# First layer's up projection by seven block products; residual added in DRAM; dense products cut 384 and 384

## The chip, the core and the metric

The kernel runs on one core of a Trainium2 chip. The metric is the device time of one execution in microseconds (us). TensorE (PE) multiplies, VectorE (DVE) and ScalarE (ACT) work elementwise, POOL and SP issue DMAs; 16 DMA engines move data between DRAM and SBUF. Matmul results land in eight PSUM banks.

## What is computed

A diffusion backbone of two layers, all in float32: 512 latent tokens (`SEQ`) and 256 context tokens (`CTX`) of width 1024. Each layer derives shift, scale and gate vectors from a conditioning vector (adaLN), norms and modulates the tokens, projects them into a convolution module, an attention and a two-way retention, gates and sums the three branches, applies `w_out`, and ends with a gated feed-forward part:

```python
def conv_ffn(h, w_up, dw_w, dw_b, w_down):
    gt, val = jnp.split(h @ w_up, 2, axis=-1)
    gt = dwconv(gt, dw_w, dw_b)          # 3 taps along the tokens
    return (jax.nn.silu(gt) * val) @ w_down
```

`w_up` is 1024 x 5632, half of it for `gt` and half for `val`; `w_down` is 2816 x 1024. In layer 0 this runs on all 768 tokens, in layer 1 on the 512 latent ones.

## The kernel before

Activations lie with features on the 128 partitions and tokens along the free dimension, one SBUF slot of 128 x 768 (`S`, 47 slots) for a block of 128 features. Every dense product takes three passes: weight and activation are split into a rounded high part and a low part (`hi`, `lo`), and `chunk` multiplies high x high, high x low and low x high into the same bank (`mm`, L197). A product over 768 tokens takes two matmuls a pass, of 512 and 256 columns, in two banks of the `pd` pool (four banks; the `ps` pool has the other four).

Weights come as one stream (`Stream`, L75): tiles of 128 x 1024, laid out by the host in the order of use. `issue` loads a raw tile on SP's queue into a ring of two buffers (`raw`; one early tile uses the pool `rawa`, whose two buffers are otherwise for modulation weights); `prepare` splits it on ScalarE (L107) and VectorE (L108), up to four tiles ahead of the one in use; `next` hands out columns.

Work that can lie beside the dense products is written as generators ("sides"). `tick` gives each side credit, the modelled time of a product times the side's rate (`ADAR` for adaLN), and the side emits instructions until the credit is used; `finish` emits the rest at once. What is emitted first has priority on its engine; the framework's scheduler lets a later instruction pass where an earlier one is not ready. `ada_rows` (L441) works out modulation vectors on VectorE: a row of 128 x 1024 weights (buffer `rowa`) is multiplied by the conditioning and summed, a pass of 768 and one of 256 columns for each of up to two vectors (L466). `ada_late` (L476) does the last piece of layer 0 and all six of layer 1; it runs beside layer 0's feed-forward part.

`last_chunks` ends a stage: its last output tiles are produced first for one half of the tokens and then for the other (512, then 256), so that `norm` (L521) of the first half can run under the second half's matmuls. `ffn` (L1420) then runs column group by column group: `up` multiplies 8 feature blocks for `gt` and 8 for `val`, `up_g` filters and applies Silu, `up_v` multiplies and splits the result into `hid`. After groups 8, 14 and 22 the down projection of finished groups is added into the residual `xs`, kept in SBUF (`evac`, L1480); the last cut is done by `last_chunks`. Layer 1 runs the same code on 512 tokens. `parts` (L67) cuts the tokens in two.

Of the kernel before, what the change touches and what calls it, by code (L numbers as in the profile page):

```python
# [14 lines left out]
F32 = mybir.dt.float32  # L16
F32R = mybir.dt.float32r
AF = mybir.ActivationFunctionType
# [4 lines left out]
P = 128  # L23
# [11 lines left out]
NSUB = 140  # L35
# [4 lines left out]
NSLOT = 47  # L40
# [5 lines left out]
ATTR, RETR, CONVR, ADAR = (1.0, 1.0), (1.4, 1.6), (0.4, 0.4), (0.06, 0.2, 0.25)  # L46
# [17 lines left out]
LAT = [(0, SEQ)]  # L64

# [9 lines left out]
class Stream:  # L75


    def __init__(self, k, dram, total):
        self.k, self.dram, self.limit = k, dram, total
        self.blocks = []  # L80
        self.raw = {}
# [40 lines left out]
    def next(self, key, cols, held=0):  # L122
        if self.off + cols > SUB:
            self.split.pop(self.cur, None)
            self.cur += 1
            self.off = 0
            self.prepare(min(self.cur - held, self.cur if self.kept is None else self.kept) + WB)
        hi, lo = self.split[self.cur]
        o = self.off
        self.off += cols  # L130
        self.blocks.append((key, cols))
        return hi[:, o:o + cols], lo[:, o:o + cols]

# [28 lines left out]
class Kern:  # L162
# [84 lines left out]
    def dense(self, key, xs, segs, ws=None):  # L247

        pts = [(self.dps()[:, :c], o, c) for o, c in segs]
# [226 lines left out]
    def ada_late(self, l):  # L476
        yield from self.ada_rows(l, LATE)
        yield from self.ada_rows(l + 1, (1, 0, 2, 3, 4, 5))
        self.crow = None
# [41 lines left out]
    def norm(self, l, which, xs, out):  # L521
# [3 lines left out]
        def gen(segs):  # L525
# [3 lines left out]
            for k in range(KC + 1):  # L529
# [5 lines left out]
                yield  # L535
        return gen
# [690 lines left out]
    def branch(self, bi, name, ys, segs, merged, ths=(), after_split=None, before_last=None):  # L1227
# [10 lines left out]
        for m in range(KC):  # L1238
# [3 lines left out]
            if m < lead:  # L1242
# [3 lines left out]
                pps = self.group([lambda k, m=m: (name, l, k * P, m * P) for m in range(lead)], yy, segs)  # L1246
            else:
                held, pps = [th], [self.dense(lambda k: (name, l, k * P, m * P), yy, segs)]
# [36 lines left out]
    def run(self):  # L1285
# [4 lines left out]
        self.W = Stream(self, io["wstream"], DEPTH * NSUB)  # L1290
        self.att_sp = [self.dram.tile([P, TALL], F32, name=f"attsp{i}") for i in range(4)]
        xsp = self.dram.tile([KC, P, SEQ], F32, name="xspill")
        first = self.start()
        xs = []
        for l in range(DEPTH):
# [8 lines left out]
            h2 = []  # L1304
            gen = self.layer_mixers(l, last, segs, T, xs, xsp, first, h2)
            xs, first = self.ffn(l, h2, xs, segs, T, gen, xsp)
# [17 lines left out]
    def layer_mixers(self, l, last, segs, T, xs, xsp, first, h2):  # L1324
# [58 lines left out]
        self.finish(mix)  # L1383
        if l == 0:
            self.finish(ada)
            ada = self.side(self.ada_rows(l, DVP), ADAR[1])
        self.branch(2, "w_pc", self.ret_out, segs, merged, ths)
# [22 lines left out]
        def evac(m, pts):  # L1410
            for pt, o, c in pts:
# [5 lines left out]
        return self.last_chunks(lambda m, k: ("w_out", l, k * P, m * P), mm, segs, HOLDO[l], evac,  # L1417
                                self.norm(l, 1, xs, h2), LEADO)

    def ffn(self, l, h2, xs, segs, T, gen, xsp):  # L1420
        nc = self.nc
        v = self.vecs[l]
        if l + 1 < DEPTH:
            ada = self.side(self.ada_late(l), ADAR[2])
        else:
            ada = None
        cuts = [(0, 6), (6, 12), (12, 17), (17, 22)]
# [51 lines left out]

        def evac(m, pts):  # L1480
# [16 lines left out]
        up_first(FIRST[l])  # L1497
        for c in range(FIRST[l], NFF):
# [7 lines left out]
            if c == NFF - 3 and l + 1 < DEPTH:  # L1506
                self.row_vectors(l + 1)
        if ada is not None:
            self.finish(ada)
# [3 lines left out]
        gen = self.last_chunks(key(3), [hid[c] for c in range(*cuts[3])], segs, HOLDD[l], evac_last, norm)  # L1513
# [134 lines left out]
```

## Time and profile before

| | |
|---|---|
| median of 3 runs | 2318.0 us (2317.86 to 2319.08) |
| profiled execution, its own time | 2320.54 us |
| its span in the trace | 2318.8 us |
| PE / DVE / ACT busy | 98% / 66% / 37% of the span |
| matmuls | 13650 |
| weight tiles (`raw<-wstream`) | 280 of 512 KB |

Busy times are unions over an engine's instructions. Matmuls overlap, so their pace is read from start to start. "Idle before" in a group is the time that the engine stood still ahead of its instructions. A row of windows gives the stretch, its length, then for each engine the busy us and the number of instructions, the granted clock, the busy share of the DMA engines and their rate. In a group, the first figure behind the bar is busy us, the second the mean length of one in ns.

### The profile page before, as it was taken

The page shows a single profiled execution, that of the slowest core. Times are in us where ns is not written, and L with a number is a line of the kernel's source. Part 1 is how long each engine was busy: PE and PEld are TensorE (multiplying, and loading weights), DVE is VectorE, ACT ScalarE, POOL GpSimd, SP SyncE. Part 2 cuts the span into 40 slices and gives each one's busy share as a digit, 9 for nine tenths or more (in the row PEclk, how much of TensorE's full clock was granted, in tenths as well). Part 3 has the DMA queues.
Part 4 walks back from the last instruction along what each step waited for, and adds up shares of the span by engine and source line. Part 5 has one row for each costly group of instructions (what it writes and reads, how often), then busy time and mean ns, then how long its engine had stood idle before and what let it go on. Part 6 is the DMA issues. An engine that isn't in the chain of part 4 may idle for free.

```text
span 2318.8 us, 34073 instructions
## 1 busy us (share of the span) xinstructions
PE 2278.0 (98%) x13650; PEld 1953.7 (84%) x13650; DVE 1536.5 (66%) x3150; ACT 866.7 (37%) x1481; POOL 28.4 (1%) x56
## 2 busy tenths in 40 slices
PE   6999999999999999999999999999999999999998
PEld 5888888888888888888888889888888889888887
DVE  6877959798774385746763359888697556544445
ACT  3465644332232242222122234565343434323233
POOL 0000000000000000000000000000000000000000
PEclk9999999999999999999999999999999999999999
DMA  7221111123242123423651121121123322322222
GB/s 286 101 74 53 44 56 46 46 82 128 100 153 84 46 100 109 134 84 110 215 200 64 64 91 65 37 74 60 55 72 110 136 83 91 109 92 99 100 92 72
DMA packets 63838, 221.54 MB, mean 96 GB/s; under 512 B 7584, under 2 KB 9904, under 8 KB 63680
## 3 DMA queue, kind: packets, MB, share of 16 engines
q1 hardware_dynamic: 59616, 203.64, 25.4%
q0 software_dynamic: 4064, 15.73, 2.0%
q8 instruction: 107, 1.75, 0.3%
q14 instruction: 51, 0.42, 0.1%
HBM read 212.53 MB, written 6.82 MB: 95 GB/s over the span
## 4 chain that ended last, share of the span: by engine, by line
PE 92%; DVE 5%; ACT 1%; issue 1%; DMA 0%; SPq 0%; DVEq 0%; ACTq 0%
PE pd L197 81%; PE ps L197 9%; PE ps L1149 2%; DVE wlo L108 1%; DVE cacc L598 1%; DVE ht L543 0%; PE ps L1062 0%; ACT whi L107 0%; DVE hl L555 0%; DMA x<-xt 0%; DVE qq L1097 0%; DVE sq L508 0%; DVE kb L752 0%; DVE mod L418 0%; DVE kf L752 0%
## 5 line engine op out<-in xcount | busy, mean ns | idle before, releaser
L197 PE MATMUL pd<-hh,wlo 128*128 128x512 f32 (+1 forms) x2176 | 658.9, 355 | 0.0
L107 ACT ACTIVATE whi<-raw 128x1024 fp32r<-128x1024 f32 x280 | 296.6, 1061 | 968.4 <-PE pd L197 849.3
L197 PE MATMUL pd<-hl,whi 128*128 128x512 f32 (+1 forms) x2176 | 655.7, 353 | 1.9 <-DVE hl L555 1.7
L197 PE MATMUL pd<-hh,whi 128*128 128x512 f32 (+1 forms) x2176 | 655.8, 354 | 1.4 <-DVE fy L1440 0.9
L108 DVE TENSOR_TENSOR wlo<-raw,whi 128x1024 fp32r<-128x1024 f32 x280 | 341.6, 1221 | 273.7 <-ACT whi L107 270.2
L197 PEld LDWEIGHTS pd<-hh,whi 128*128 128x128 f32 x2176 | 362.0, 189 | 63.2 <-issue 1.5
L197 PEld LDWEIGHTS pd<-hl,whi 128*128 128x128 f32 x2176 | 359.7, 188 | 61.4 <-DVE hl L555 3.8
L197 PEld LDWEIGHTS pd<-hh,wlo 128*128 128x128 f32 x2176 | 360.3, 188 | 56.0 <-issue 1.1
L598 DVE SCALAR_TENSOR_TENSOR cacc<-u,vec,cacc 128x497 f32<-128x497 f32 (+9 forms) x360 | 220.3, 648 | 2.2
L197 PE MATMUL pd<-hidh,wlo 128*128 128x512 f32 (+1 forms) x558 | 169.1, 348 | 0.0
L197 PE MATMUL pd<-hidh,whi 128*128 128x512 f32 (+1 forms) x558 | 167.9, 346 | 0.0
L197 PE MATMUL pd<-hidl,whi 128*128 128x512 f32 (+1 forms) x558 | 167.3, 345 | 0.0
L1132 ACT ACTIVATE prob<-ps,amx,qrs 128x256 f32<-128x256 f32 (+1 forms) x144 | 93.7, 655 | 91.4 <-DVE amx L1127 78.3
L197 PE MATMUL pd<-whi,hl 128*128 128x256 f32 x416 | 120.1, 289 | 4.4 <-DVE hl L555 4.4
L197 PE MATMUL pd<-whi,hh 128*128 128x256 f32 x416 | 120.5, 292 | 3.4 <-ACT hh L552 3.4
L197 PE MATMUL pd<-wlo,hh 128*128 128x256 f32 x416 | 119.5, 288 | 0.0
L1483 DVE SCALAR_TENSOR_TENSOR x<-pd,mod,x 128x512 f32<-128x512 f32 (+1 forms) x102 | 62.2, 632 | 80.8 <-PE pd L197 80.5
L466 DVE SCALAR_TENSOR_TENSOR rowa<-rowa,crow 128x768 f32<-128x768 f32 (+1 forms) x144 | 94.1, 686 | 26.8 <-DMA rowa<-wadt 26.7
L197 PEld LDWEIGHTS pd<-hidh,whi 128*128 128x128 f32 x558 | 94.9, 189 | 14.9 <-issue 0.2
L1448 DVE TENSOR_TENSOR fy<-fy,pd 128x512 f32<-128x512 f32 x66 | 37.5, 596 | 104.6 <-PE pd L197 101.5
L197 PEld LDWEIGHTS pd<-hidl,whi 128*128 128x128 f32 x558 | 93.7, 188 | 14.0 <-issue 0.2
L197 PEld LDWEIGHTS pd<-hidh,wlo 128*128 128x128 f32 x558 | 94.3, 189 | 13.1
(245 smaller groups left out, 3111.9 us busy)
## 6 DMA issues: line engine op xcount, KB each, us to landing
raw<-wstream SPq DMA_DIRECT2D x280, 512.0 KB, 3.4
rowa<-wadt SPq DMA_DIRECT2D x72, 512.0 KB, 3.7
adar<-wada SPq DMA_DIRECT2D x16, 384.0 KB, 7.3
rawa<-wada SPq DMA_DIRECT2D x8, 512.0 KB, 3.5
x<-xt SPq DMA_DIRECT2D x8, 384.0 KB, 8.1
x<-xt POOLq DMA_DIRECT2D x8, 384.0 KB, 5.1
adar<-wada SPq DMA_DIRECT2D x8, 256.0 KB, 7.0
xspill<-x POOLq DMA_DIRECT2D x8, 256.0 KB, 2.3
```

Source lines behind the costliest of these rows:

```text
L107: nc.scalar.activation(hi, r, AF.Copy)
L108: nc.vector.tensor_tensor(lo, r, hi.bitcast(F32), op=ALU.subtract)
L197: return self.nc.tensor.matmul(out, w, x, start=start, stop=stop)
L466: nc.vector.scalar_tensor_tensor(out, raw[:, a:b], 1.0, t[:, o:o + b - a], op0=ALU.mult, op1=ALU.mult, accum_out=acc[:, c, j, h:h + 1])
L598: nc.vector.scalar_tensor_tensor(acc[:, a:b], u[:, a + d:b + d], w(k), acc[:, a:b], op0=ALU.mult, op1=ALU.add)
L1132: nc.scalar.activation(pr[:, o - k0:o - k0 + c], pt[:, :c], AF.Exp, scale=rs, bias=mx[:, 2:3], accum_out=sm[:, j:j + 1])
L1149: nc.tensor.transpose(pt[:, b * P:b * P + P], pr[:, o + b * P:o + b * P + P], self.ident)
L1448: nc.vector.tensor_tensor(y[:, o:o + n], y[:, o:o + n], pt, op=ALU.mult)
L1483: nc.vector.scalar_tensor_tensor(xs[m][:, s], pt, g2[:, m, j:j + 1], xs[m][:, s], op0=ALU.mult, op1=ALU.add)
```

## The change

Layer 0's up projection is taken as a product of 2 x 2 blocks: features halved (512 each), tokens halved (384 each), and the output columns of one group halved into `gt` and `val`. Winograd's form of Strassen's scheme makes seven products in place of eight, of sums and differences of blocks. `split_tokens` makes the seven token operands, each split into high and low: 28 slots. The weight operands are made per column group: the stream holds each product's first block, and the further blocks of a sum are added into the raw tile by accumulating DMAs from a second array (`wsums`, on POOL's queue) or on VectorE from another raw tile (`up_sums`). Each product is 4 x 3 matmuls of 384 columns; X collects 11, S2, S3 and 22 one behind the other and is copied out in between, Z collects S1 and S4. Six products (11 and 12 of three groups) come before the first that needs the second token half.

The stream of layer 0 grows from 140 to 173 tiles; odd tiles of the up projection use the `rawa` buffers. The residual is stored to DRAM (`xup`), the down projection's cuts are scaled into a slot and added there by accumulating DMAs, and the sum is loaded again ahead of the last cut, which has 6 groups for 5. The modulation pieces of `ada_late` go beside `w_out` of layer 0 (layer 0's last piece and two of layer 1) and beside the branches of layer 1 (its other four). The input, gate, branch and output projections and the down cuts of layer 0 take 384 + 384 columns (`even`); the last cut keeps 512 + 256.

```diff
-NSUB = 140
+NUP = 74
+NSUB = (NUP + NFF * 7 // 2 + NFF, 140)
 START = ((0, 256, 2), (256, 256, 0), (512, 256, 4), (768, 256, 0))
 ND = 4
 RAWB, RAWA = 2, 2
 WB = 4
-NSLOT = 47
+NSLOT = 48
...
-ATTR, RETR, CONVR, ADAR = (1.0, 1.0), (1.4, 1.6), (0.4, 0.4), (0.06, 0.2, 0.25)
+ATTR, RETR, CONVR, ADAR = (1.0, 1.0), (1.4, 1.6), (0.4, 0.4), (0.06, 0.25, 0.35, 0.6)
...
+HALF = TALL // 2
+EVEN = [(0, HALF), (HALF, HALF)]
+Q = 4 * P
...
+OPS = {"11": ((0, 0),), "12": ((0, 1),), "22": ((1, 1),), "S1": ((1, 0), (1, 1)), "S3": ((0, 0), (1, 0)),
+       "S2": ((0, 0), (1, 0), (1, 1)), "S4": ((0, 1), (0, 0), (1, 0), (1, 1))}
+UPFIRST = 3
+CUTS = ((0, 4), (4, 8), (8, 12), (12, 16), (16, NFF))
+CUTAT = {5: 0, 9: 1, 13: 2, 17: 3}
+def up_order():
+    first = range(UPFIRST)
...
+    for c in range(UPFIRST, NFF):
+        out += [("11", c), ("22", c - 1), ("S4", c - 1), None, ("12", c), ("S2", c), ("S1", c), ("S3", c)]
+    return out + [("22", NFF - 1), ("S4", NFF - 1)]
...
+def up_sums():
...
+    for (name, c), (i, o) in tile.items():
+        blocks = OPS[name]
+        other = {"S2": "S1", "S4": "S2"}.get(name)
+        if other and abs(tile[other, c][0] - i) <= 3:
+            dve.setdefault(i, []).append((o, *tile[other, c]))
+        else:
+            dma.setdefault(i, []).extend((o, (c, b)) for b in blocks[1:])
+    return dma, dve
...
-            pool, tag = (self.k.apool, "rawa") if i == RAWB else (self.k.raw_pool, "raw")
+            ada = i == RAWB or (NUP < i < NSUB[0] and i % 2)
+            pool, tag = (self.k.apool, "rawa") if ada else (self.k.raw_pool, "raw")
             t = pool.tile([P, SUB], F32, tag=tag, name=f"raw{i}")
             self.k.nc.sync.dma_start(t, self.dram[i])
+            for o, block in self.dma.get(i, ()):
+                self.k.nc.gpsimd.dma_start(t[:, o:o + Q], self.sums[len(self.sum_blocks)], accum_op=ALU.add)
+                self.sum_blocks.append(block)
...
-            self.issue(i + 1)
-            r = self.raw.pop(i)
+            up = NUP <= i < NSUB[0]
+            self.issue(i + 2 if up else i + 1)
+            r = self.raw[i]
+            for o, j, a in self.dve.get(i, ()):
+                nc.vector.tensor_tensor(r[:, o:o + Q], r[:, o:o + Q], self.raw[j][:, a:a + Q], op=ALU.add)
+            self.raw.pop(i - 4, None)
...
-            self.issue(self.done + RAWB)
+            self.issue(self.done + (RAWB + 1 if up else RAWB))
...
-        return self.dense(lambda k: ("w_in", l, k * P, m * P), self.h, segs)
+        return self.dense(lambda k: ("w_in", l, k * P, m * P), self.h, even(segs))
...
+    def ada_late(self, l, parts):
+        for x in parts:
+            yield from self.ada_rows(l, x)
+            l += 1
...
+    def split_tokens(self, l, xs, ops):
...
+        def block(name, i, half, k0, segs):
+            cf, sh = self.coef[l], self.mod[l]
+            t = raw[name, i] = self.S("b")
+            for e in range(2):
+                k = k0 + 2 * i + e
+                for o, c in spans(segs):
+                    j, d = o // SEQ, slice(e * HALF + o - half, e * HALF + o - half + c)
+                    nc.vector.scalar_tensor_tensor(t[:, d], xs[k][:, o:o + c], cf[:, KC + k, j:j + 1], r[:, o:o + c],
+                                                   op0=ALU.mult, op1=ALU.mult)
+                    nc.scalar.activation(t[:, d], t[:, d], AF.Identity, bias=sh[:, 24 + k, j:j + 1])
+        def parts(name, t, i):
+            ops.setdefault(name, [None, None])[i] = self.split(t, TALL, "h")
+        def gen(segs):
+            half = segs[0][0]
+            self.sq_rstd(segs, r)
+            yield
+            if not half:
+                for name, k0 in (("11", 0), ("12", 4)):
+                    for i in range(2):
+                        block(name, i, half, k0, segs)
+                        yield
+                        parts(name, raw[name, i], i)
+                        yield
+                return
...
+            for i in range(2):
+                for name, k0 in (("u", 0), ("v", 4)):
+                    block(name, i, half, k0, segs)
+                    yield
+                u, v, b = raw["u", i], raw["v", i], raw["11", i]
+                t3[i], t2[i] = self.S("t3"), self.S("t2")
+                nc.vector.tensor_tensor(t3[i], v, u, op=ALU.subtract)
+                nc.vector.scalar_tensor_tensor(t2[i], t3[i], -1.0, b, op0=ALU.mult, op1=ALU.subtract)
+                yield
+                parts("S2", t2[i], i)
+                yield
...
+            ada = self.side(self.ada_late(l, [(2, 3, 4, 5)]), ADAR[2])
...
+            late = self.side(self.ada_late(l, [LATE, (1, 0)]), ADAR[3])
...
+        norm = self.norm(l, 1, xs, h2) if last else self.split_tokens(l, xs, h2)
+        gen = self.last_chunks(lambda m, k: ("w_out", l, k * P, m * P), mm, even(segs), HOLDO[l], evac, norm, LEADO)
+        if late:
+            self.finish(late)
...
+        cuts = [(0, 6), (6, 12), (12, 17), (17, 22)] if l else CUTS
...
+        def up_seven():
+            X, Z, g, val = {}, {}, {}, {}
+            def product(pt, name, c, start=True):
+                wh, wl = self.W.next(("up", c, OPS[name][0]), Q)
+                for k in range(4):
+                    xh, xl = (a[:, k % 2 * HALF:(k % 2 + 1) * HALF] for a in h2[name][k // 2])
+                    b = slice(k * P, k * P + P)
+                    for i, (w, x) in enumerate(((wh, xh), (wh, xl), (wl, xh))):
+                        nc.tensor.matmul(pt, w[:, b], x, start=start and k == 0 and i == 0, stop=k == 3 and i == 2,
+                                         skip_group_check=not start)
+            one, two = slice(0, HALF), slice(HALF, TALL)
+            def p11(c):
+                X[c], g[c], val[c] = self.dps()[:, :HALF], self.S("fg"), self.S("fv")
+                product(X[c], "11", c)
+                nc.scalar.activation(g[c][:, one], X[c], AF.Copy)
...
+            def s2(c):
+                product(X[c], "S2", c, False)
+                nc.scalar.activation(g[c][:, two], X[c], AF.Copy)
+            def s1(c):
+                Z[c] = (self.ps() if 0 < c < UPFIRST else self.dps())[:, :HALF]
+                product(Z[c], "S1", c)
+            def s3(c):
+                product(X[c], "S3", c, False)
+                nc.scalar.activation(val[c][:, two], X[c], AF.Copy, scale=-1.0)
+                nc.vector.tensor_tensor(val[c][:, two], val[c][:, two], Z[c], op=ALU.subtract)
+            def p22(c):
+                product(X[c], "22", c, False)
+                nc.scalar.activation(val[c][:, one], X.pop(c), AF.Copy, scale=-1.0)
+            def s4(c):
+                product(Z[c], "S4", c, False)
+                gc = g.pop(c)
+                nc.vector.tensor_tensor(gc[:, two], gc[:, two], Z.pop(c), op=ALU.add)
...
+                nc.scalar.activation(y, y, AF.Silu)
+                vc = val.pop(c)
+                nc.vector.tensor_tensor(vc, vc, y, op=ALU.mult)
+                hid[c] = self.split(vc, T, "hid")
...
+            n, c, started = 0, UPFIRST, False
+            for x in up_order():
+                if x is None:
+                    if c in CUTAT:
+                        down(CUTAT[c])
+                    c += 1
+                    continue
+                if x[0] == "S2" and not started:
+                    started = True
+                    for _ in gen:
+                        pass
+                    xs.clear()
+                steps[x[0]](x[1])
+                n += 1
+                if n == 1:
+                    next(gen)
+        def down(p):
+            for m in range(KC):
+                t = self.S("dx")
+                pts = self.dense(lambda k: key(p)(m, k), [hid[c] for c in range(*cuts[p])], EVEN, None, self.ps)
+                for pt, o, c in kinds(pts):
+                    nc.scalar.activation(t[:, o:o + c], pt, AF.Copy, scale=g2[:, m, o // SEQ:o // SEQ + 1])
+                nc.gpsimd.dma_start(xup[m], t, accum_op=ALU.add)
...
-        up_first(FIRST[l])
-        for c in range(FIRST[l], NFF):
+        if l == 0:
+            for k in range(KC):
+                nc.sync.dma_start(xup[k], xs[k])
+            up_seven()
+            h2.clear()
+            for k in range(KC):
+                xs.append(self.S("x"))
+                nc.gpsimd.dma_start(xs[k], xup[k])
+            self.row_vectors(l + 1)
+        else:
+            up_first(FIRST[l])
...
+        gen = self.last_chunks(key(-1), [hid[c] for c in range(*cuts[-1])], segs, HOLDD[l], evac_last, norm)
```

## Rows read from the trace of the kernel before

**Rows 1.** The page: busy times, and the chain by line (share of the span).

```profile
PE 2278.0 (98%) x13650; PEld 1953.7 (84%) x13650; DVE 1536.5 (66%) x3150; ACT 866.7 (37%) x1481; POOL 28.4 (1%) x56
...
PE pd L197 81%; PE ps L197 9%; PE ps L1149 2%; DVE wlo L108 1%; DVE cacc L598 1%; DVE ht L543 0%; PE ps L1062 0%; ACT whi L107 0%; DVE hl L555 0%; DMA x<-xt 0%; DVE qq L1097 0%; DVE sq L508 0%; DVE kb L752 0%; DVE mod L418 0%; DVE kf L752 0%
```

**Rows 2.** Windows: us; busy of PE, PEld, DVE, ACT, POOL; clock; DMA share, GB/s.

```profile
727.00:819.00 92.00, 92.00 (x523) 80.08 (x522) 40.67 (x55) 28.18 (x36) 0.00 (x0) 1.00 0.17 58
820.00:850.00 30.00, 26.72 (x144) 21.72 (x143) 27.28 (x53) 15.46 (x26) 0.00 (x0) 1.00 0.27 88
850.00:1380.00 530.00, 530.00 (x2986) 458.73 (x2984) 296.41 (x611) 131.21 (x156) 5.92 (x11) 1.00 0.35 119
1380.00:1400.00 20.00, 17.20 (x123) 16.16 (x123) 17.84 (x28) 10.70 (x16) 0.00 (x0) 0.91 0.21 79
1720.00:1760.00 40.00, 40.00 (x178) 33.04 (x177) 38.17 (x52) 10.86 (x13) 2.16 (x4) 1.00 0.37 121
1760.00:1936.00 176.00, 176.00 (x831) 147.57 (x830) 91.15 (x120) 63.25 (x83) 4.25 (x8) 1.00 0.30 105
```

**Rows 3.** Timeline of TensorE, up projection: start, length in us.

```profile
900.28 0.51 PE L197 MATMUL pd<-hl,whi 128*128 128x512 f32 x2
...
903.46 0.51 PE L197 MATMUL pd<-hl,whi 128*128 128x512 f32 x2
```

**Rows 4.** Chain in order of time: start, us, what.

```profile
71.44 2.88 PE pd L197 x24
...
464.90 137.52 PE pd L197 x793
...
603.71 25.43 PE pd L197 x144
```

**Rows 5.** Timeline of TensorE, layer 1, 512 columns alone.

```profile
2100.22 0.39 PE L197 MATMUL pd<-hh,whi 128*128 128x512 f32 x1
...
2102.94 0.39 PE L197 MATMUL pd<-hh,whi 128*128 128x512 f32 x1
```

**Rows 6.** Timeline of VectorE, modulation rows one behind the other.

```profile
1116.43 0.95 DVE L466 SCALAR_TENSOR_TENSOR rowa<-rowa,crow 128x768 f32<-128x768 f32 x1
...
1117.65 0.96 DVE L466 SCALAR_TENSOR_TENSOR rowa<-rowa,crow 128x768 f32<-128x768 f32 x1
```

**Rows 7.** Timeline of TensorE: first matmul behind the output projection.

```profile
818.86 0.40 PE L197 MATMUL pd<-hh,whi 128*128 128x512 f32 x1
```

**Rows 8.** DMA issues: size of one, median us from issue to landing.

```profile
raw<-wstream SPq DMA_DIRECT2D x280, 512.0 KB, 3.4
rowa<-wadt SPq DMA_DIRECT2D x72, 512.0 KB, 3.7
...
x<-xt SPq DMA_DIRECT2D x8, 384.0 KB, 8.1
x<-xt POOLq DMA_DIRECT2D x8, 384.0 KB, 5.1
...
rl<-attsp POOLq DMA_DIRECT2D x4, 256.0 KB, 4.0
```

**Rows 9.** VectorE groups by form, 690 to 1390 us.

```profile
L108 DVE TENSOR_TENSOR wlo<-raw,whi 128x1024 fp32r<-128x1024 f32 x82 | 100.0, 1220 | 84.8 <-ACT whi L107 84.8
...
L1438 DVE SCALAR_TENSOR_TENSOR fy<-pd,vec,fy 128x511 f32<-128x511 f32 x22 | 16.4, 745 | 30.8 <-ACT fy L1436 30.8
...
L1448 DVE TENSOR_TENSOR fy<-fy,pd 128x512 f32<-128x512 f32 x22 | 15.1, 688 | 64.4 <-PE pd L197 63.3 <-ACT fy L1442 1.1
...
L1438 DVE SCALAR_TENSOR_TENSOR fy<-pd,vec,fy 128x255 f32<-128x255 f32 x22 | 10.4, 473 | 0.0
```

**Rows 10.** ScalarE groups by form, the same stretch.

```profile
L107 ACT ACTIVATE whi<-raw 128x1024 fp32r<-128x1024 f32 x82 | 87.0, 1061 | 390.1 <-PE pd L197 368.1 <-issue 21.4 <-DMA raw<-wstream 0.5
...
L1442 ACT ACTIVATE fy<-fy 128x768 f32<-128x768 f32 x22 | 18.6, 847 | 50.2 <-DVE fy L1440 50.1
L1436 ACT ACTIVATE fy<-pd,vec 128x512 f32<-128x512 f32 x22 | 16.8, 762 | 0.0
```

More of the change, by code (lines that the diff above doesn't have):

```diff
@@ L64, with even, kinds, spans @@
 LAT = [(0, SEQ)]
+HALF = TALL // 2
+EVEN = [(0, HALF), (HALF, HALF)]
+Q = 4 * P
+def even(segs):
+    return EVEN if len(segs) > 1 else segs
+def kinds(pts):
+    for pt, o, c in pts:
+        a = max(0, min(c, SEQ - o))
+        if a:
+            yield pt[:, :a], o, a
+        if a < c:
+            yield pt[:, a:c], o + a, c - a
+def spans(segs):
+    for o, c in segs:
+        a = max(0, min(c, SEQ - o))
+        yield from [(o, a)] * (a > 0) + [(o + a, c - a)] * (a < c)
+OPS = {"11": ((0, 0),), "12": ((0, 1),), "22": ((1, 1),), "S1": ((1, 0), (1, 1)), "S3": ((0, 0), (1, 0)),
[5 more added lines that the diff above has]
+    first = range(UPFIRST)
+    out = [(n, c) for c in first for n in ("11", "12")] + [(n, c) for n in ("S2", "S1", "S3") for c in first]
+    for c in range(UPFIRST - 1):
+        out += [("22", c), ("S4", c)]
+    for c in range(UPFIRST, NFF):
+        out += [("11", c), ("22", c - 1), ("S4", c - 1), None, ("12", c), ("S2", c), ("S1", c), ("S3", c)]
+    return out + [("22", NFF - 1), ("S4", NFF - 1)]
+def up_sums():
+    tile, cuts, n, c = {}, 0, 0, UPFIRST
+    for x in up_order():
+        if x is None:
+            if c in CUTAT:
+                assert n % 2 == 0
+                a, b = CUTS[CUTAT[c]]
+                cuts += b - a
+            c += 1
+            continue
+        tile[x] = (NUP + cuts + n // 2, Q * (n % 2))
+        n += 1
+    dma, dve = {}, {}
+    for (name, c), (i, o) in tile.items():
[6 more added lines that the diff above has]
+    return dma, dve
 def parts(segs):
@@ L130, in next, with up_blocks @@
         self.off += cols
-        self.blocks.append((key, cols))
+        if key[0] == "up":
+            self.blocks.extend((b, P) for b in up_blocks(*key[1:]))
+        else:
+            self.blocks.append((key, cols))
         return hi[:, o:o + cols], lo[:, o:o + cols]
+def up_blocks(c, block):
+    row, half = block
+    return [("w_up", 0, (4 * half + j) * P, row * DFF + c * P) for j in range(4)]
 class Side:
@@ L1289, in run @@
         self.setup()
-        self.W = Stream(self, io["wstream"], DEPTH * NSUB)
+        self.W = Stream(self, io["wstream"], io["wsums"], sum(NSUB))
         self.att_sp = [self.dram.tile([P, TALL], F32, name=f"attsp{i}") for i in range(4)]
         xsp = self.dram.tile([KC, P, SEQ], F32, name="xspill")
+        xup = [self.dram.tile([P, TALL], F32, name=f"xup{k}") for k in range(KC)]
         first = self.start()
@@ L1303, in run @@
                     self.row_vectors(l)
-            h2 = []
+            h2 = [] if last else {}
             gen = self.layer_mixers(l, last, segs, T, xs, xsp, first, h2)
-            xs, first = self.ffn(l, h2, xs, segs, T, gen, xsp)
+            xs, first = self.ffn(l, h2, xs, segs, T, gen, xsp, xup)
     def out_norm(self, xs):
@@ L1383, in layer_mixers @@
         self.finish(mix)
+        late = None
         if l == 0:
@@ L1415, in evac, with ffn @@
             self.sq_add(m, xs[m], [(o, c) for _, o, c in pts], m == KC - 1)
-        return self.last_chunks(lambda m, k: ("w_out", l, k * P, m * P), mm, segs, HOLDO[l], evac,
-                                self.norm(l, 1, xs, h2), LEADO)
-    def ffn(self, l, h2, xs, segs, T, gen, xsp):
+        norm = self.norm(l, 1, xs, h2) if last else self.split_tokens(l, xs, h2)
+        gen = self.last_chunks(lambda m, k: ("w_out", l, k * P, m * P), mm, even(segs), HOLDO[l], evac, norm, LEADO)
+        if late:
+            self.finish(late)
+        return gen
+    def ffn(self, l, h2, xs, segs, T, gen, xsp, xup):
         nc = self.nc
         v = self.vecs[l]
[L1423 to L1427, printed above, removed]
+        cuts = [(0, 6), (6, 12), (12, 17), (17, 22)] if l else CUTS
         after = {8: [0], 14: [1], 22: [2]}
@@ L1505, in ffn @@
                     del hid[i]
[L1506 to L1509, printed above, removed]
         h2.clear()
@@ L1638 @@
         k.run()
-    arrays["wstream"] = _blocks(k.W.blocks, a, DEPTH * NSUB)
+    arrays["wstream"] = _blocks(k.W.blocks, a, sum(NSUB))
+    arrays["wsums"] = np.stack([np.concatenate([a[n][l, r:r + P, c:c + P] for n, l, r, c in up_blocks(*b)], 1)
+                                for b in k.W.sum_blocks])
     wada = np.zeros((NADA, P, SUB), np.float32)
```

70 lines of the change are left out of this document (58 added, 12 removed).

## The prediction

> **What bounds the kernel now.** I read the page first. TensorE is busy 98% of the span, and 81% of the chain that ended last is one line, the matmul in `mm` writing the `pd` banks [rows 1]. The windows say the same of the stage that changes: from 850 to 1380 us, the feed-forward part of layer 0, TensorE is busy 530 us of 530 [rows 2]. A matmul removed there counts in full unless something else then ends later. The profiled execution took 2320.5 us (span 2318.8), the median of the runs is 2318.0: I make the sum against 2320.5 and take 2.5 us off at the end.
>
> Then the timeline, for the pace of matmuls from start to start, since ends overlap.
> - 512 + 256 columns, up projection: nine pairs in 3.18 us, 353.3 ns a pair [rows 3].
> - The same pair elsewhere, from the chain in order of time: 793 matmuls in 137.52 us, 346.8 ns a pair, near 465 us; 144 in 25.43, 353.2, in the gates near 604. 256 columns alone, near 71 us: 24 in 2.88, 120.0 ns [rows 4].
> - 512 alone, layer 1: twelve in 2.72 us, 226.7 ns [rows 5].
> 512/2.4 is 213.3 and 256/2.4 is 106.7 ns, so each matmul costs its columns at 2.4 GHz (granted clock 1.00) and some 13.3 ns, the mixed pair sometimes 6.7 more.
>
> **The seven products.** Before: 22 column groups x 2 halves x 8 x 3 passes = 1056 pairs x 353.3 = 373.1 us. After: 22 x 7 products x 4 x 3 = 1848 matmuls of 384 columns. No row shows 384 columns. Between the two uniform streams lies 173.3 ns (346.7 a pair); below it 3/4 of the 512 pace, 170.0; above it half the slow pair, 176.7. I take 173.3, since both streams lie on one line: 320.3 us, 52.8 saved (46.6 to 58.9).
>
> The Trainium skill, "TensorE: Matmul & The Clock Gate", section "Back-to-back issue gap", gives columns/2.4 + 2.5 ns for a warm matmul, almost no fixed cost. By it the pairs would be 343.3 and the products 300.3 us, 43 saved, and equal cuts would gain nothing. The trace disagrees (226.7 against its 215.8 ns), so the sum stays with the rows.
>
> **Equal cuts elsewhere.** The first 16 chunks of the down projection, 16 x 8 x 3 = 384 pairs, and the gates and branch products from 600 to 740 us, some 390, run at 353.3 now. At 346.7 they give 774 x 6.67 ns = 5.2 us. Ends: nothing, if 384 + 384 settles at 353.3 too; 3.9 us lost, if the 400 pairs from 460 to 600 and the 192 of `w_out` rise to it; 9 gained, if the 600 or so beside attention gain as well. The evacuations, in three pieces for two, lie under matmuls.
>
> **Where the modulation goes.** `ada_late` leaves the feed-forward part. Three of its seven pieces (`LATE`, and two for layer 1) go beside `w_out`: 24 rows, each with two pairs of VectorE passes at 1.22 us a pair [rows 6], 58.6 us. From 727 to 819 us, which reaches to the end of `w_out` [rows 7], VectorE is busy 40.7 of 92 us [rows 2], so 51 are free, and the norm of the first token half, with its splits, moves some 9 us in. About 16 us of rows are left over when `w_out` ends, 32 if they can't start before 750. `finish(late)` emits the rest of them ahead of the second half's norm, which is therefore queued behind them on VectorE. Two `rawa` buffers pace them too: (2.4 + 3.7 + 0.4)/2 = 3.3 us a row [rows 8]; and the odd weight tiles of the new loop live in these buffers, so weights (S3 of the third group) queue behind rows.
>
> Then the second half is normed and combined before S2 can run. A block is four multiplies and four ScalarE shifts; two blocks, a difference, a sum and a split are 5.3 us of VectorE per i by its passes of 1 us for 768 columns and 0.47 for 255 [rows 6, 9]; both i, two or three weight splits of 1.22 and the adds of p12 make 16, behind 4 of row statistics. What covers it are six products, 72 x 173.3 ns = 12.5 us. If the rows in front hold VectorE, S2 is late by 16 + 20 - 12.5 = 23 us, 39 with 32 left over; if buffers hold the rows instead, by some 9, and up to 16 come back where the weight tile behind them is due. I take 20, ends 9 and 39. An idle stretch can cost clock besides: from 1380 to 1400 us TensorE was idle 2.8 us and the granted clock averaged 0.91, some 3.6 us at 1.2 GHz, worth 1.8; that is inside the ends. Today's stall at this place, 3.3 us of idle TensorE from 820 to 850 [rows 2], goes. Net +16.7 us.
>
> The other four pieces run beside layer 1's branches: 32 x 1.22 = 39 us of VectorE. It is 95% busy up to 1760, with no TensorE idle, and then 91 of 176 us to 1936 [rows 2], 85 free. I take 1 us; nothing at best, 8 if the convolution's end is pushed into branch 0.
>
> **Inside the loop of seven.** A group lasts 7 x 12 x 173.3 ns = 14.6 us. VectorE: 3.5 weight splits x 1.22, four filter taps 2.4, product and low part 1.9, three 384-column adds near 0.56, 41/22 weight sums x 0.69: 11.5 us, 79% [rows 6, 9]. ScalarE: 3.5 x 1.06, four bank copies near 0.66 (under the 0.76 of 512 columns), three passes of 0.85: 8.9 us, 61% [rows 10]. Both fit. But S3 may not write X before ScalarE has copied S2's result out, with only S1 (2.08 us) between, and 22 stands so behind S3: a copy of 0.66 with one weight split of 1.06 ahead of it passes, with two it does not, and behind the late copy wait the next copies and splits. I take 0.3 us on each of 19 groups, 5.7; nothing at best, 1.5 each (28) if the queues usually meet so.
>
> Weight sums: 53 accumulating DMAs of 256 KB by POOL and 41 adds on VectorE. No row shows an accumulate. POOL's reads of this size land in 4.0 us, the slowest transfer listed takes 8.1 [rows 8]. Traffic is 2.4 MB in 14.6 us, 165 GB/s; DMA was 37% busy at 121 [rows 2], so about half. In odd groups S4 adds a tile three places back, and the buffer which that add frees is loaded anew: split 3.0 + load 3.4 + accumulate x + add and split 3.0 must fit four tiles of 4.16 us, so x may be 7.2. At 4.0, which I take, it costs nothing; at 8.1 about 1 us in every other group, 9 in all.
>
> **Residual in DRAM.** Eight stores of 384 KB on SP's queue, 32 accumulates and eight reloads (5.1 us each [rows 8]) on POOL's. Nobody waits for the accumulates, and the weight sums queued behind them are issued seven tiles ahead. The reloads need slots, which come free from product 11 of the last group on, 12 us before its end. The last down cut follows at once on the last group, whose filter, Silu and split take about 9 us, while two output tiles hold 10.6 us of other chunks: 2 us, ends 0 and 6.
>
> **Sum.** -52.8 - 5.2 + 16.7 + 5.7 + 1 + 2 = -32.6: 2287.9, by the runs' median 2285.4. I say 2286.
>
> **Rivals.**
> 1. *The boundary is covered.* If rows fill VectorE's gaps before `w_out` ends, S2 waits some 7 us for today's 3.3 and the loop never: 2318 - 52.8 - 5.2 + 4 + 1 = 2265. For: VectorE is under half busy from 727 on. Against: 58.6 + 9 us into 51, through two buffers. Chance 0.18.
> 2. *Queues meet in the loop*: 1.5 us a group, 22 over my sum: 2308. For: 79% and 61% with 2.08 us to spare. Against: from 850 to 1380 the same engines empty TensorE's banks and it is never idle. Chance 0.16.
> 3. *Weight sums come late*, the slower side. An accumulate reads its target and writes it, so x may exceed a plain transfer's. Each us over 7.2 stalls nine or ten groups, and as the split stands in ScalarE's and VectorE's order, bank copies wait with it. It turns the sum at x = 10.6; at 12 it makes 4.8 x 9.5 = 46: 2331. Against: no median in the list is over 8.1. Chance 0.12.
> 4. *Equal cuts gain nothing and 384 columns take 176.7 ns*, the mixed pair's surplus being no matter of its mixture: 6.2 and 5.2 us less gain, 2297. For: the pair shows both paces. Against: both uniform streams carry 13.3 ns. Chance 0.04. By the rule of the Trainium skill above, 43 saved and nothing from cuts, it would be 2300.
>
> My forecast, 2270 to 2302, has 0.50. **Range:** 2260 to 2320 leaves out the best of the first rival and most of the third, 0.17 in all. About 0.2% (4.6 us) is what a measurement of this kernel can tell from no change. Faster holds the forecast, 1, 4 and most of 2: 0.81; same, the edges of 2 and 3: 0.05; slower, the rest of both and a boundary past its end: 0.14.
>
> **What would show it.** In the changed profile: 384-column matmuls 173.3 ns apart; TensorE idle of 9 to 39 us between the sixth product and S3 of the third group, with modulation rows on VectorE there; no idle over a few tenths of a us in later groups; accumulating POOL issues landing under 7 us. A pace over 176.7, S2 prompt after the sixth product, or idle in every group would prove steps of mine wrong.

## The result, and the profile after

The changed kernel takes 2393.6 us (median of 4 runs, 2392.6 to 2400.5) against 2317.9 of the kernel before: ratio 1.033, interval 1.031 to 1.036. It is 75.7 us slower where I forecast 32 us faster, and beyond my range's upper end of 2320. The profiled execution's span is 2391.3 us.

The page of the kernel after: busy times, and the chain's shares by engine. They answer to [rows 1].

```profile
PE 2244.9 (94%) x13386; PEld 2045.1 (86%) x13386; DVE 1620.5 (68%) x3248; ACT 982.4 (41%) x1701; POOL 108.2 (5%) x152
...
PE 75%; DVE 11%; DMA 8%; issue 4%; ACT 3%; SPq 0%; DVEq 0%; POOLq 0%; POOL 0%; ACTq 0%
```

TensorE issues 264 matmuls fewer and is busy 33 us less, but it now holds 75% of the chain: VectorE and transfers have a fifth of it.

Windows of the kernel after (columns as in [rows 2]): up to the end of the output projection, five of the boundary, one of the loop of seven, and layer 1's branches.

```profile
727.00:819.00 92.00, 88.71 (x503) 86.74 (x501) 63.13 (x144) 26.22 (x33) 0.90 (x1) 1.00 0.41 140
820.00:850.00 30.00, 16.61 (x74) 14.61 (x74) 18.75 (x39) 11.27 (x17) 3.48 (x4) 0.82 0.44 112
850.00:875.00 25.00, 1.65 (x2) 0.50 (x2) 18.67 (x55) 3.54 (x7) 4.31 (x5) 0.50 0.86 234
875.00:900.00 25.00, 0.00 (x0) 0.00 (x0) 19.72 (x58) 2.98 (x8) 2.59 (x3) 0.50 0.59 165
900.00:925.00 25.00, 22.52 (x111) 21.59 (x112) 21.17 (x29) 16.89 (x28) 3.47 (x4) 0.86 0.38 90
...
819.00:925.00 106.00, 40.78 (x187) 36.70 (x188) 79.32 (x180) 34.67 (x59) 13.85 (x16) 0.68 0.57 150
925.00:1300.00 375.00, 346.87 (x1920) 342.00 (x1919) 189.30 (x246) 170.54 (x260) 47.44 (x55) 0.96 0.57 142
...
1760.00:1936.00 176.00, 169.30 (x780) 138.07 (x778) 156.28 (x308) 66.24 (x86) 7.98 (x15) 1.00 0.58 200
```

Three stretches lose where [rows 2] lost next to nothing. Right behind the output projection TensorE is idle 65 us of 106. In the loop, at 173.3 ns a matmul, 375 us hold 2163 matmuls and 1920 were started: 42 us lost, 28 of them idle and the rest a granted clock of 0.96. In layer 1's branches it is idle 6.7 of 176 us. In none of the three is VectorE full; it waits too.

Waits of TensorE in the kernel after: 800 to 925 us, then 925 to 1400 us (in all, times, longest).

```profile
PE pd L1655 <- ACT hh L415: 56.3, 4, 47.8
PE ps L289 <- ACT sqt L597: 9.4, 1, 9.4
...
PE pd L1655 <- ACT fg L1672: 14.9, 8, 2.8
PE ps L289 <- ACT dx L1728: 13.5, 5, 3.5
PE pd L1655 <- ACT fg L1663: 4.8, 1, 4.8
```

The 47.8 us are S2 of the first group waiting for its token operand. Below it, the loop's waits are all for ScalarE, never for a weight tile, although the weights cause them, as the next view shows.

Timeline of VectorE, ScalarE and TensorE in the loop, kernel after: start, length, what, [idle before <- releaser].

```profile
1023.25 0.55 DVE L1681 TENSOR_TENSOR fv<-fv,pd 128x384 f32<-128x384 f32 x1
1029.10 0.69 DVE L186 TENSOR_TENSOR raw<-raw,raw 128x512 f32<-128x512 f32 x1 [5.31 <-DMA raw<-wsums]
...
1030.85 0.55 DVE L1690 TENSOR_TENSOR fg<-fg,pd 128x384 f32<-128x384 f32 x1
...
1031.43 1.03 ACT L1693 ACTIVATE fy<-fg,vec 128x768 f32<-128x768 f32 x1 [4.82 <-DVE fg L1690]
...
1035.54 0.47 ACT L1672 ACTIVATE fg<-pd 128x384 f32<-128x384 f32 x1
...
1036.06 0.45 PE L1655 MATMUL pd<-hh,whi 128*128 128x384 f32 x1 [2.48 <-ACT fg L1672]
...
1037.46 0.52 PE L1655 MATMUL pd<-hh,whi 128*128 128x384 f32 x1
1037.78 0.52 PE L1655 MATMUL pd<-hl,whi 128*128 128x384 f32 x1
```

Read it downwards. VectorE stands 5.31 us at the add that completes S2's weight sum, waiting for the accumulate into the next tile. Behind it stands the add that feeds the previous group's filter, so ScalarE idles 4.82 us at `fy`; behind `fy`, in ScalarE's order, stands the copy of S2's bank, and S3 waits 2.48 us for that. The weight that all this waits for isn't used until 1048 us. Right behind the pause TensorE's granted clock is 0.50, the level of 1.2 GHz:

```profile
1037.00:1040.00 3.00, 3.00 (x11) 3.00 (x10) 2.77 (x4) 1.22 (x2) 0.00 (x0) 0.50 0.37 116
```

Ten matmuls then start 320 ns apart in place of 173, 1.5 us more, so that the pause of 2.5 us costs nearly 4. By the Trainium skill, "TensorE: Matmul & The Clock Gate", section "Back-to-back issue gap", a cold matmul costs columns/1.2 ns, which for 384 columns is 320 ns; the trace agrees.

### The profile page after: what moved, and what is told of

Its sections match the earlier page's. It is cut to its first block, busy times and chain, and to the rows that moved or that the text cites. A ratio compares the mean times of both kernels' runs of the same rounds, so it can differ in the third digit from the quotient of the medians.

```text
span 2391.3 us, 34285 instructions
## 1 busy us (share of the span) xinstructions
PE 2244.9 (94%) x13386; PEld 2045.1 (86%) x13386; DVE 1620.5 (68%) x3248; ACT 982.4 (41%) x1701; POOL 108.2 (5%) x152
## 4 chain that ended last, share of the span: by engine, by line
PE 75%; DVE 11%; DMA 8%; issue 4%; ACT 3%; SPq 0%; DVEq 0%; POOLq 0%; POOL 0%; ACTq 0%
PE pd L289 53%; PE ps L289 13%; PE pd L1655 5%; DMA rowa<-wadt 3%; DMA raw<-wsums 3%; DVE wlo L191 2%; PE ps L1309 2%; DMA raw<-wstream 1%; DVE rowa L558 1%; ACT whi L190 1%; PE ps L1655 1%; DVE junk L558 1%; DVE fy L1695 1%; PE ps L1222 0%; DVE fy L1697 0%
## 5 line engine op out<-in xcount | busy, mean ns | idle before, releaser
L289 PE MATMUL pd<-hh,whi 128*128 128x384 f32 (+2 forms) x1472 | 471.5, 360 | 5.0 <-DVE sg L1424 5.0
L289 PE MATMUL pd<-hh,wlo 128*128 128x384 f32 (+2 forms) x1472 | 470.7, 359 | 0.0
L289 PE MATMUL pd<-hl,whi 128*128 128x384 f32 (+2 forms) x1472 | 470.3, 360 | 0.0
L289 PEld LDWEIGHTS pd<-hh,wlo 128*128 128x128 f32 x1472 | 271.9, 188 | 26.1 <-issue 1.1
L1655 PE MATMUL pd<-hh,whi 128*128 128x384 f32 x512 | 175.0, 345 | 76.1 <-ACT hh L415 56.3
L1655 PE MATMUL pd<-hl,whi 128*128 128x384 f32 x512 | 174.9, 342 | 0.2 <-DVE hl L416 0.2
L1655 PE MATMUL pd<-hh,wlo 128*128 128x384 f32 x512 | 174.5, 341 | 0.0
L289 PE MATMUL pd<-hidh,whi 128*128 128x512 f32 (+1 forms) x302 | 103.5, 354 | 0.6 <-DVE x L1736 0.5
L289 PE MATMUL pd<-hidl,whi 128*128 128x512 f32 (+1 forms) x302 | 102.6, 351 | 0.0
L289 PE MATMUL pd<-hidh,wlo 128*128 128x512 f32 (+1 forms) x302 | 102.4, 351 | 0.0
```

What stands on the lines that cost most here:

```text
L289: return self.nc.tensor.matmul(out, w, x, start=start, stop=stop)
L1655: nc.tensor.matmul(pt, w[:, b], x, start=start and k == 0 and i == 0, stop=k == 3 and i == 2, skip_group_check=not start)
```

## The experiments

Theory A: the boundary, modulation rows ahead of the second half's norm, costs most. Theory B: the weight sums in the loop do.

**e1_no_late, e1b_no_late: no late rows.**

```diff
-            late = self.side(self.ada_late(l, [LATE, (1, 0)]), ADAR[3])
+            (constants into mod and, in e1b, coef; crow dropped)
```

> Leaves out the 24 modulation rows beside layer 0's output projection (pieces LATE of layer 0, (1, 0) of layer 1); constants stand in their place, so the values are not the reference's. Theory A, most of the loss is the boundary, rows on VectorE ahead of the second half's norm: TensorE's 73 us of idle from 800 to 925 us fall to about 10, the run to about 2393.6 - 63 = 2331 (2320 to 2340). Theory B, the loss is mainly in the loop of seven (weight sums, queues) and the boundary would be covered by other waits: less than 30 us come back, 2365 or more.

Measured 2361.2 us, and misleading: a product of my constants with a layer 1 vector was scheduled ahead of everything, and VectorE stood 26.5 us at its load before the first matmul.

> As e1_no_late, but the stand-in constants are written into the modulation and coefficient tiles directly, so that VectorE waits for no vector load at the start (in e1_no_late it stood 26.5 us there, and branch 0 began 26 us later). Theory A (rows ahead of the second half's norm cost about 58 us): 2335 (2328 to 2343). Theory B (the boundary costs what e1_no_late showed as a whole, 32 us): 2355 or more.

Measured 2335.7 us (2330.1 to 2338.2), 58 less, as theory A has it.

```profile
819.00:925.00 106.00, 90.87 (x473) 87.73 (x473) 79.57 (x115) 58.90 (x89) 15.59 (x18) 0.90 0.61 151
925.00:1300.00 375.00, 348.88 (x1934) 344.04 (x1933) 175.03 (x225) 165.81 (x261) 53.63 (x62) 0.97 0.62 148
```

The same windows: the boundary's idle time falls from 65 to 15 us, the loop is as bad as it was (1934 matmuls). So the two losses are separate.

**e2_no_sums: the 53 accumulating transfers left out.**

```diff
-  self.k.nc.gpsimd.dma_start(t[:, o:o + Q], self.sums[...], accum_op=ALU.add)
```

> Leaves out the 53 accumulating DMAs of the weight sums (the transfers alone; the 41 adds on VectorE stay), so some weights lack a term. Theory A (boundary): the boundary stays, and only the 35 us of idle in the loop of seven can go; at most 30 come back, 2363 or more. Theory B (sums landing late hold ScalarE's and VectorE's order): 25 to 40 us come back, 2354 to 2369, and the idle of some 7.5 us in each period of four groups falls under 2. Theory C (the bank copies alone): under 8 us come back, 2386 or more.

Measured 2333.1 us (2331.4 to 2335.6): 60 less, more than either theory gave.

```profile
819.00:925.00 106.00, 53.89 (x264) 50.45 (x265) 87.48 (x190) 42.77 (x69) 0.00 (x0) 0.74 0.35 118
925.00:1300.00 375.00, 374.90 (x2155) 372.76 (x2154) 204.06 (x264) 186.70 (x289) 27.30 (x32) 1.00 0.53 138
```

In the loop 2155 matmuls start, which is full pace; the boundary, where VectorE also stood at adds, gives back some 13 us (264 matmuls from 819 to 925 us, from 187). Both theories are true of one part each; the bank copies alone (theory C) cost nothing.

**e7_one_load, e16_after_norm: what about the rows costs?** The first loads 3 row blocks in place of 24 and makes all passes; the second moves the left-over rows behind the norm.

```diff
-                raw = ...; nc.sync.dma_start(raw, self.io["wadt"][l, 8 * pc + c])
+                if c == 0 or (l, pc) not in ((0, 5), (1, 0), (1, 1)): (the same)   # e7
...
+                    self.finish(self.late)      # e16: behind the second half's norm, in up_seven
-            self.finish(late)                   # e16: at the end of layer_mixers
```

> All 24 rows beside the output projection keep their VectorE passes, but each piece loads its first row block only and passes over it eight times (3 loads for 24), so the values are not the reference's. Theory A1 (VectorE's passes alone hold the norm): rows still start where they start now, the run stays within 5 us of 2393.6. Theory A2 (the rows are paced by their two buffers, 3.9 us a row from 850 to 893 us against 2.44 of passes): 11 rows x 1.4 us = 16 us come back there and some more before 817 us, 2365 to 2378.

Measured 2386.1 us, 7.5 less. Neither answer: the left-over rows now run in 20 us (eight, from 860 to 879) in place of 39, but the wait for S2 is still 48 us. The edit isn't clean: a row block now keeps its buffer for eight rows of passes, the weight tile that shares the buffer is loaded only at 844 us, and VectorE stands at that tile's add. TensorE's wait for S2 and VectorE's at the add:

```profile
PE pd L1656 <- ACT hh L415: 52.4, 4, 48.4
...
852.55 0.69 DVE L186 TENSOR_TENSOR raw<-raw,raw 128x512 f32<-128x512 f32 x1 [7.75 <-DMA raw<-wsums]
```

So how much of the rows' cost is passes and how much is buffers stays open.

> The changed kernel with one line moved: the rows that are left over when the output projection ends are worked off behind the second half's norm and its splits in place of ahead of it. Same rows, same rate, same buffers. Theory A (place ahead of the norm): the wait for S2 of 48 us falls under 15, and 25 to 45 us come back, 2349 to 2369. Rival (the work itself, 12 rows of 2.44 us of VectorE and weight tiles queued behind them in the shared buffers, costs wherever it stands): the wait turns up at S1 or S3 and under 15 us come back, 2379 or more.

Measured 2400.1 us: my theory fell, the rival holds.

```profile
PE pd L1654 <- ACT hh L415: 23.6, 4, 14.4
PE pd L1654 <- DVE fv L1680: 15.6, 1, 15.6
PE ps L289 <- ACT sqt L597: 9.9, 1, 9.9
PE ps L1654 <- ACT whi L190: 8.9, 1, 8.9
```

TensorE's waits from 800 to 960 us: the wait for S2 shrinks to 14.4 us, and the rows then hold VectorE's subtraction of S1's bank (15.6) and, in the shared buffers, a weight tile (8.9). Only where the rows aren't in the stretch at all does their time come back.

**e6_early: the same rows beside the branches.**

```diff
-            ada = self.side(self.ada_rows(l, DVP), ADAR[1])       # 0.25
+            ada = self.side(self.ada_early(l), ADAR[1])           # DVP, LATE, (1, 0); 0.5
-            late = self.side(self.ada_late(l, [LATE, (1, 0)]), ADAR[3])
```

> The same rows, moved: one side works off pieces (2, 3), LATE and layer 1's (1, 0) beside the three branch products, at rate 0.5 in place of 0.25, and nothing of them stands beside the output projection; the result is the reference's. Theory A: VectorE has room there (it was busy 12.9 of 25 us from 740 to 765) and the run gains what e1b gains, 2328 to 2343. Rival: two row buffers and VectorE's queue delay the branches' merges, the branch stage grows by 10 to 30 us from 270, and the run stays at 2345 to 2365.

Measured 2348.3 us: the rival's figure. The boundary is free of rows, but rows delay the convolution, whose end branch 0 needs: the output projection starts at 762 us in place of 747.

**e10_order, e12_place, e11_both: the loop, with all transfers kept.**

```diff
-  None, ("12", c), ("S2", c), ("S1", c), ("S3", c)
+  None, ("S1", c), ("S2", c), ("12", c), ("S3", c)      # e10, e11 (with e6)
-  nc.vector.tensor_tensor(r[...], r[...], self.raw[j][...], op=ALU.add)
+  with self.k.after(self.lo): (the same add)             # e12: behind the low part before
```

> In the loop of seven the order 12, S2, S1, S3 becomes S1, S2, 12, S3, so that S1's summed tile stands at or ahead of S2's; transfers, adds and products stay 53, 41 and 154, and the boundary stays. Theory A (the loop's 35 us come from place: the add for S2 stands at VectorE's head, waiting for the accumulate into the next tile, and bank copies behind it): 20 to 35 us come back, 2359 to 2374. Theory B (the transfers themselves are too slow for four buffers, 4.4 us of load and 5.3 of accumulate): the splits still wait, within 8 us of 2393.6. Theory C (the new order is worse: 12's add on VectorE and S2's copy on ScalarE now fall together): 2394 or more.

Measured 2368.8 us (2361.2 to 2376.1), 25 less: the time of theory A. The loop starts 2068 matmuls in 375 us.

> The changed kernel with one constraint on VectorE's order: the 41 adds that complete a weight sum are issued behind the low part of the weight tile before, in place of up to three splits ahead of it (in e11_both the add of one tile stood 5.3 us ahead of the low parts of the two tiles before it). Order of the products as in the changed kernel. Theory A (place in VectorE's order, not the transfer's duration): 12 to 30 us come back, 2364 to 2381. Theory B (an accumulate of 5.3 us behind a load of 4.4 is too long for four buffers wherever the add stands): within 6 us of 2393.6; worse if the low parts then wait as well.

Measured 2386.9 us (2378.2 to 2389.7), 7 less: between the theories. The profiled execution, the fastest of the four, starts 2017 matmuls. With S2 ahead of S1 the add still needs the next tile's accumulate.

> e6_early and e10_order together. If the two losses are separate, the gains add: 2393.6 - 58 - 28 = 2308 (2295 to 2322), under the 2318 of the kernel before. If either theory falls, 2335 or more.

Measured 2323.8 us (2318.5 to 2329.0), 70 less than the changed kernel and just above the range: the gains of e6_early (45) and e10_order (25) add. What was left in the loop is seen on VectorE (timeline of e11_both):

```profile
966.41 0.55 DVE L1670 TENSOR_TENSOR fg<-fg,ps 128x384 f32<-128x384 f32 x1
972.25 0.69 DVE L186 TENSOR_TENSOR raw<-raw 128x512 f32<-128x512 f32 x1 [5.29 <-DMA raw<-wsums]
972.86 1.22 DVE L191 TENSOR_TENSOR wlo<-raw,whi 128x1024 fp32r<-128x1024 f32 x1
974.00 0.55 DVE L1683 TENSOR_TENSOR fv<-fv,pd 128x384 f32<-128x384 f32 x1
974.46 1.22 DVE L191 TENSOR_TENSOR wlo<-raw,whi 128x1024 fp32r<-128x1024 f32 x1
```

Counted off in order, the add is that of tile 103, and the two low parts behind it are those of 101 and 102. It was put two tiles too early.

**e13_conv: order, place, and rows from the convolution's end on.** What is left of the rows after branch 0 goes on beside the output projection.

```diff
  (e10_order and e12_place; ADAR 0.27 for 0.25 beside the branches; and)
         self.finish(conv)
+        if l == 0:
+            self.finish(ada)
+            late = self.side(self.ada_late(l, [LATE, (1, 0)]), ADAR[3])   # 0.75
+            ada = None
...
-        if l == 0:
-            late = self.side(self.ada_late(l, [LATE, (1, 0)]), ADAR[3])   # 0.6
```

> Three changes of place: product order of e10_order, the adds' place of e12_place, and the late rows start when the convolution has ended, beside branch 0, at rate 0.75, in place of beside the output projection. The result is the reference's. If the losses are boundary, add place and (in e6_early) rows pushing the convolution's end: branch stage back at 270 us from 287, loop idle under 10 us: 2323.8 - 16 - 8 = 2300 (2290 to 2308), under the 2320 of the kernel before. If rows still stand ahead of the norm: 2315 or more.

Measured 2294.6 us (2291.7 to 2298.3), ratio to the kernel before 0.990, interval 0.988 to 0.991. Windows:

```profile
819.00:925.00 106.00, 96.53 (x520) 93.25 (x519) 86.42 (x125) 66.65 (x102) 19.32 (x23) 0.94 0.69 166
925.00:1300.00 375.00, 375.00 (x2163) 373.59 (x2162) 201.13 (x259) 182.23 (x282) 58.97 (x73) 1.00 0.71 171
```

In the loop TensorE is busy 375.00 of 375 us with 2163 matmuls, 173.4 ns each, every transfer, add and copy still there. VectorE's waits at the adds from 925 to 1300 us are down to one of 1.2 us. Here they are in the kernel after, in e2_no_sums and in e13_conv (in all, times, longest):

```profile
DVE raw L186 <- DMA raw<-wsums: 56.4, 13, 6.2
DVE raw L186 <- DMA raw<-wstream: 19.5, 4, 7.8
...
DVE raw L185 <- DMA raw<-wstream: 52.6, 14, 8.0
...
DVE raw L187 <- DMA raw<-wsums: 1.2, 1, 1.2
```

TensorE doesn't pay for the sum of these waits. In e2_no_sums VectorE stands 52.6 us at adds for plain loads and TensorE waits for nothing; in e10_order it stands 90 us, as in the changed kernel, and TensorE idles 10 us for 28; in e12_place it stands 36 us and TensorE still idles 16. Which work stands behind the add must count too, but no run varies that alone. Of the runs that keep all transfers, only the one with order and place together (and the rows moved) has a loop without idle time.

**e17_all: e13_conv without the accumulates** (the edit of e2_no_sums).

> e13_conv without the 53 accumulating DMAs (some weights lack a term). Theory: with the adds in place the transfers fit their buffers, and taking them away gives nothing in the loop; 2294.6 within 5 us. Rival: they still hold buffers at the boundary or in the first groups, 5 to 20 us come back, 2275 to 2290.

Measured 2291.3 us, 3 less: the transfers, once the adds stand right, cost about that much.

**e5b_no_l1, e14_l1, e15_rate: layer 1's rows.**

```diff
-            ada = self.side(self.ada_late(l, [(2, 3, 4, 5)]), ADAR[2])    # 0.35
+            ada = None; (constants)                                       # e5b
+            ada = self.side(self.ada_rows(l, (2, 3, 4)), ADAR[2])         # e14; e15: 0.26
+            ada = self.side(self.ada_late(l, [(5,)]), 0.25)               # e14, e15: in ffn
```

> The changed kernel without layer 1's four pieces beside its branches (32 rows left out; constants stand in their place, written directly into the tiles). Theory: they cause the 9 us by which the stretch from layer 0's last down product to the end grew (924.3 to 933.6): 2385 (2382 to 2388). Rival: equal cuts, queues or clock there: 2390 or more.

Measured 2386.3 us, 7.2 less: these rows cost what the stretch had grown by, nearly.

> e13_conv with layer 1's piece 5 moved from beside layer 1's branches into its feed-forward part (8 of 32 rows). Theory: layer 1's branches are 8 to 10 us late because rows stand on VectorE ahead of merges; with a quarter of the rows gone 2 to 5 us come back against e13_conv. Rival: the last quarter is in nobody's way, no difference (within 2 us).

Measured 2295.0 us: the rival; a quarter fewer rows at the same density change nothing.

> e14_l1 with layer 1's remaining 24 rows fed at 0.26 in place of 0.35, so thinner over the three branches. Theory (rows fed densely stand ahead of a merge and its gate, one wait of 5 us at 1839 us and a slow clock behind it): 3 to 8 us come back, 2287 to 2292. Rival: rows reach further into branch 0 and the output projection, no gain or a few us lost, 2294 to 2299.

Measured 2287.7 us (2286.8 to 2294.3), ratio to the kernel before 0.987, interval 0.986 to 0.989: the fastest version here, 30 us under the kernel before. Density counted, though one of the four runs lies among those of e14_l1.

**e3_even: equal cuts alone, on the kernel before.**

```diff
-  self.dense(..., segs)
+  self.dense(..., even(segs))      # in win, branch, and the down chunks of up to cut 2
```

> The kernel before with one part of the change alone: gates, branch products and the first 16 chunks of the down projection of layer 0 take 384 and 384 columns in place of 512 and 256. By the prediction's term: 774 pairs or more at 346.7 in place of 353.3 ns, 5.2 us less, 2313 (2309 to 2314). Rival: no gain, 2318, or up to 4 us lost, 2322, if 384 + 384 costs what the slow mixed pair costs.

Measured 2309.3 us, ratio 0.995 (0.994 to 0.997): 11 us less than the runs beside it, twice the term.

## Why the prediction was wrong, step by step

- **The seven products: right.** The 384-column matmuls stand 173.3 ns apart wherever nothing waits; the fixed 13.3 ns a matmul held, and rival 4 is out. By the rule of the Trainium skill that the prediction weighed ("TensorE: Matmul & The Clock Gate", section "Back-to-back issue gap": columns/2.4 + 2.5) it would be 162.5 ns; the trace disagrees, as [rows 5] did.
- **Equal cuts: right sign, about the size.** 5.2 taken, 11 measured in e3_even. But some 4.5 of the 11 come from pairs of the up projection that no edit touched (last section), and the changed kernel has no such pairs: some 6 are the cuts' own.
- **Where the modulation goes: the step that failed first.** I took 20 us (ends 9 and 39); without the rows 58 come back. The prices were right: passes of a row again 1.22 us a pair, loads 4.2 us for 3.7. The quantity and the queue were wrong. I set 58.6 us of rows against 51 us of free VectorE time and took 16 us as left over. But a side is fed only as its rate and the ticks allow: the first pass starts at 768 us, 21 us into the stage, and 53 of 96 passes start from 816.6 us on, 13 rows or 32 us. That was my upper end, and still not the cost, because I let one thing wait for one other. In fact VectorE also stood 6.3 us at an add for a weight tile whose buffer a row still held, rows then came at 3.6 us (11 from 853 to 892) in place of 2.44, and the norm came last; and my end of 39 held no clock at half speed, though I wrote that it did (16 + 36 - 12.5 = 39.5 without it): of the 74 us lost from 819 to 925 (187 matmuls at 173.3 ns in 106 us) 65 were idle and 8 the clock. e16_after_norm shows that it wasn't the place ahead of the norm alone, which I had named as the cause.
- **Layer 1's pieces:** 1 taken, 8 the end, 7.2 measured.
- **Inside the loop: the bank copies cost nothing, the weight sums were wrong.** In e2_no_sums and e13_conv every copy, split and tap is there and TensorE runs at full pace, so the load of the two engines fits, and the 5.7 us that I took for the copies aren't seen. The failed sentence is that an accumulate may take 7.2 us and cost nothing at 4.0. It took 5.3 (median of 53, 256 KB), within my slack, and the loop lost 48 us from 925 to 1380 (2347 matmuls in 455 us). I asked whether a tile's sum is ready when TensorE needs the tile, and it was, with 14 us to spare and more. I didn't ask who waits for it earlier. The add for S2 reads the next tile in the stream (in every second group; else its own), adds stand in VectorE's order up to three splits ahead of their own tile's, and the bank additions behind a waiting add wait as well. Rival 3 had the right engine order (bank copies behind a late split) and the wrong condition: it was to turn the sum at 10.6 us a transfer, and did so at 5.3. By the Trainium skill, "PSUM — Partial Sum Buffer", section "Engine vs sequencer instructions", the queues of ScalarE and VectorE are strictly first in, first out; the timeline above agrees, with 5.31 us at the add and nothing passing it.
- **Residual in DRAM: not tried by itself.** Its 32 accumulates landed in 6.2 us, and in e13_conv the same traffic leaves the loop without idle time, so there its cost can be little. The reloads landed in 8.6 us where I took 5.1, yet of the 2 us that I took for the last cut TensorE waits 0.5 (kernel after, 1375 to 1449 us).
- **The sum.** 53 and 6 us gained, 58, 48 and 7 lost by these steps, and the boundary's own 12 (15 us idle without rows, for 3.3 before): 66 slower. Measured are 76; the other 10 no single run accounts for. The two profiles say where the time lies: from the last matmul of the output projection to layer 0's last down product it is 631.5 us for 566.8, 65 more, which is what 53 gained, 70 lost at the boundary (74 for 3.3) and 48 in the loop make; the stretch behind it is 9 longer, and it begins 1.4 earlier: 72.5 in all, as the two spans differ.

The first rival (boundary covered, loop never waiting, 2265) is what e15_rate comes near: a loop that is busy 374.4 of 375 us, a boundary with 10.8 us of idle time left, and 23 us above it.

## What to carry to other kernels

An asynchronous sum has two consumers: the engine that uses the data, and the in-order engine whose instruction waits for it first. Price the wait at the second, by what stands behind it and what that has to spare. And work that is moved into free time fits by the hour it is fed, not by the total: count what is left over at the stage's end from the rate that feeds it, then let everything queue behind that, buffers included.

## What the hardware showed that was not expected

An accumulating transfer on POOL's queue landed in 5.3 us for 256 KB and 6.2 us for 384 KB, against 3.5 for plain loads of 512 KB on SP's queue, all medians of the kernel after:

```profile
raw<-wstream SPq DMA_DIRECT2D x313, 512.0 KB, 3.5
...
raw<-wsums POOLq DMA_DIRECT2D x53, 256.0 KB, 5.3
xup<-dx POOLq DMA_DIRECT2D x32, 384.0 KB, 6.2
```

In e3_even pairs of 512 and 256 columns that no edit touched changed their pace. Timeline of TensorE there, before and after the first down chunk of equal cuts:

```profile
900.10 0.51 PE L212 MATMUL pd<-hh,whi 128*128 128x512 f32 x2
...
903.28 0.51 PE L212 MATMUL pd<-hh,whi 128*128 128x512 f32 x2
...
1060.31 0.51 PE L212 MATMUL pd<-hh,whi 128*128 128x512 f32 x2
...
1063.43 0.51 PE L212 MATMUL pd<-hh,whi 128*128 128x512 f32 x2
```

Nine pairs took 3.18 us, 353.3 ns each as in [rows 3], and later 3.12 us, 346.7 each. Some 670 pairs ran at the second pace, worth 4.5 us, most of what the term of the cuts lacked. What switches it stays open.
